# Both tiles of queries of a head pair in one attention step, with the softmax inverses on GpSimd

## The chip, the cores and the metric

The kernel runs on one core of one Trainium2 chip. The metric is the device time of one execution in microseconds (us), lower is better; each kernel is run several times and the median counts. One execution is also recorded by the hardware profiler, and its rows are what this document argues from. The engines are named as the profile names them: PE is TensorE (matmuls), PEld its weight loads, DVE is VectorE, ACT is ScalarE, POOL is GpSimd, SP issues nearly all DMAs.

## The reference

The program is a small encoder trunk: 256 tokens, model width 1024, two layers, float32 inputs. An even layer mixes two kinds of attention behind one input projection; the odd layer uses dilated windows. Each is followed by a squared-ReLU MLP. The change touches the attention of the even layer:

```python
def even_mixer(xn, w_in, rpb, q_norm, w_uq, kv_norm, w_ukv, w_o, cos_r, sin_r):
    hcat = xn @ w_in
    ...
    out_a = neighbourhood_attention(a_qkv[:, :, 0], a_qkv[:, :, 1], a_qkv[:, :, 2], rpb)
    ...
    out_b = dense_attention(q, k, v, (MLA_NOPE + MLA_ROPE) ** -0.5)
    return jnp.concatenate([out_a, out_b], axis=-1) @ w_o
```

Both kinds have 8 heads. In the first (neighbourhood attention, head width 64) a query sees a window of the 4 x 64 grid and a learned bias is added to its scores. The second (latent attention) is dense, with queries and keys of width 96 and values of width 64. For both, each row of scores passes through a softmax:

```python
sc = jnp.einsum('bqhd,bkhd->bhqk', qi, k, preferred_element_type=jnp.float32) * scale
p = jax.nn.softmax(sc, axis=-1)
return jnp.einsum('bhqk,bkhd->bqhd', p.astype(v.dtype), v)
```

## The kernel before

Activations lie as columns of tokens (256 tokens, two tiles of 128). A float32 product is made of three matmuls of a rounded type: every operand is split into a high part and the rest (`split`, L167 a cast on ScalarE, L168 a difference on VectorE), and `mm3` (L171 to L173) multiplies high by high, high by low and low by high. All weights are read from memory once, 1 MB pieces at a time, on SP's queue, and split in quarters (`whi`, `wlo`) up to two weights ahead of their use. So ScalarE and VectorE have a steady load of splits beside everything else.

The even layer's attention is woven into the projections around it. `attention` returns a list of side steps; the loop at the end of `even` runs the main steps (queries and keys of head pairs 1 to 3, the latent queries, keys and values, and the output projection) and after each of them as many side steps as its share of cost allows. This order, as written, is what the scheduling layer starts from; it then sets each engine's order, moving an instruction back where it does not expect its operands in time. Each engine runs its order strictly.

There are 16 items: kind 0 (neighbourhood) and then kind 1 (latent), for each of four head pairs, for each of two tiles of queries. One item passes through three functions:

- `scores`: the scores of two heads into PSUM banks of tag `w` (of which there are four). Kind 0 uses `two_heads` (L180): the two heads have 64 rows each and sit side by side in the array; each takes a bank of its own of which half is used. Kind 1 uses `mm3`. Then, on VectorE, one instruction a head scales the scores, adds the bias (kind 0, L668; kind 1 has none, L671) and takes the minimum of their negation; on ScalarE one exp a head with its sum `z` (L673); on VectorE the inverse of both sums (L674); on ScalarE one scaling a head (L676).
- `turn_probs`: four transpositions on TensorE (L683) into a bank, and a copy out of it (L685, on ScalarE or VectorE).
- `mix`: the products with the values (L697), two heads in halves of 64 columns of the array, into a bank, then a `split` of 128 columns for the output projection.

The side steps of the items are set in the order scores(n), turn_probs(n - 1), mix(n - 2), with two empty steps after the first scores. So an item's transpositions are the fourth side step behind its scores, and its mix comes four behind them.

The bias of an item (256 KB) is loaded by `load_bias` into one of two buffers, two items ahead; its DMA waits on SP's queue until the item that had the buffer has read it.

Of the kernel before, what the change touches and what calls it, by code (L numbers as in the profile page):

```python
# [16 lines left out]
F32 = mybir.dt.float32  # L17
F32R = mybir.dt.float32r
AF = mybir.ActivationFunctionType
ALU = mybir.AluOpType  # L20
# [3 lines left out]
P = 128  # L24
D = 1024
KT = D // P
T = 256
NT = T // P
# [5 lines left out]
MLA_SCALE = (64 + 32) ** -0.5  # L34
# [4 lines left out]
SPLIT_AHEAD = 2  # L39
WPARTS = 4  # L40
NORM_PRIO = 300


@with_exitstack
def trunk(ctx, tc, a, out):
    nc = tc.nc
# [123 lines left out]
    def mm3(o, sh, sl, mh, ml, first, last):  # L170
        nc.tensor.matmul(o, sh, mh, start=first, stop=False)  # L171
        nc.tensor.matmul(o, sh, ml, start=False, stop=False)  # L172
        nc.tensor.matmul(o, sl, mh, start=False, stop=last)  # L173

    def two_heads(o, hi, lo, ts):

        for n, (y, z) in enumerate(((hi, hi), (hi, lo), (lo, hi))):
            for j in range(2):
                pb = slice(64 * j, 64 * j + 64)
                nc.tensor.matmul(o[j], y[pb, 0, ts], z[pb, 1, :], start=n == 0, stop=n == 2)  # L180
# [10 lines left out]
    def tok(t):  # L191
        return slice(t * P, (t + 1) * P)
# [255 lines left out]
    def even(ep):  # L448
# [200 lines left out]

        def scores(n):  # L650
            kind, t, hp = items[n]
            load_bias(n + 2)

            sb = [bank("w")[:, 0:T] for _ in range(2)] if kind == 0 else bank("w").rearrange("p (j n) -> p j n", j=2)
            s_of = lambda j: sb[j] if kind == 0 else sb[:, j]
            if kind == 0:
                two_heads(sb, *qk[hp], tok(t))
            else:
                for j in range(2):
                    h = 2 * hp + j  # L660
                    (qh, ql), (kh, kl) = mT["q"], mT["k"]
                    mm3(sb[:, j], qh[0:96, h, tok(t)], ql[0:96, h, tok(t)], kh[0:96, h, :], kl[0:96, h, :], True, True)
            pp, sn = scratch([2, T], "pp"), scratch([2, T], "sn")
            mn, z, rz = (work.tile([P, 2], F32, tag=v, name=v, bufs=3) for v in ("mn", "z", "rz"))
            for j in range(2):
                o = s_of(j)
                if kind == 0:
                    nc.vector.tensor_tensor_reduce(out=sn[:, j], in0=o, in1=biases[n][:, j, :], op0=ALU.add, op1=ALU.min,  # L668
                                                   scale=-1.0, scalar=3e38, accum_out=mn[:, j:j + 1])
                else:  # L670
                    nc.vector.tensor_scalar(sn[:, j], o, -MLA_SCALE, None, ALU.mult, ALU.min, accum_out=mn[:, j:j + 1])  # L671
            for j in range(2):
                nc.scalar.activation(pp[:, j], sn[:, j], AF.Exp, bias=mn[:, j:j + 1], scale=-1.0, accum_out=z[:, j:j + 1])  # L673
            nc.vector.reciprocal(rz, z)  # L674
            for j in range(2):
                nc.scalar.activation(pp[:, j], pp[:, j], AF.Copy, scale=rz[:, j:j + 1])  # L676
            probs[n] = pp

        def turn_probs(n):
            pp = probs.pop(n)  # L680
            pt = bank("w")
            for b in range(4):
                nc.tensor.transpose(pt[:, b * P:(b + 1) * P], pp[:, b // 2, (b % 2) * P:(b % 2 + 1) * P], ident)  # L683
            turned[n] = scratch([4, P], "pts")
            nc.any.tensor_copy(out=turned[n], in_=pt.rearrange("p (b n) -> p b n", b=4))  # L685

        def mix(n):
            kind, t, hp = items[n]
            pts = turned.pop(n)
# [4 lines left out]
            for kk in range(NT):  # L694
                for j in range(2):
                    h = 2 * hp + j
                    nc.tensor.matmul(pvo[64 * j:64 * j + 64, 0:P], v[:, kk, h * 64:(h + 1) * 64], pts[:, 2 * j + kk, :],  # L697
                                     start=kk == 0, stop=kk == NT - 1)
            split(*(z[:, hp, tok(t)] for z in mixed[kind]), pvo[:, 0:P])

        def attention():

            out = []
            for n in range(len(items) + 2):
                for fn, m in ((scores, n), (turn_probs, n - 1), (mix, n - 2)):
                    if 0 <= m < len(items):
                        out.append(lambda fn=fn, m=m: fn(m))
                if n == 0:
                    out += [lambda: None] * 2
            return out  # L710

        (ug, ut), (kg, kt) = uq_steps(), ukv_steps()
        first = qk_steps(0)
        run_all(first[:1])
        load_bias(0)
        load_bias(1)
        run_all(first[1:3])
        row = as_row(dg)
        nc.scalar.mul(both[:, 0, :], row, HD ** -0.5)
# [230 lines left out]
def _layout(i):  # L950
    f = np.ascontiguousarray
    w = i["ev_w_in"][0]
    d = {"x": f(i["x"][0][ORDER].T.reshape(KT, P, T).transpose(1, 0, 2))}
    d["w_c"] = f(w[:, 1536:].reshape(2, 4, P, 416).transpose(0, 2, 1, 3).reshape(2, P, -1))
    d["w_qk"] = f(w[:, :1024].reshape(KT, P, 2, 4, P).transpose(3, 1, 0, 2, 4).reshape(4, P, -1))
    d["w_v"] = f(w[:, 1024:1536].reshape(2, 4, P, 512).transpose(0, 2, 1, 3).reshape(2, P, -1))
    d["w_uq"] = f(i["ev_w_uq"][0].reshape(1, 2, P, 768).transpose(0, 2, 1, 3).reshape(1, P, -1))
    d["w_ukv"] = f(i["ev_w_ukv"][0].reshape(1, P, 1024))
    d["w_oe"] = f(i["ev_w_o"][0].reshape(4, 2, P, D).transpose(0, 2, 1, 3).reshape(4, P, -1))
    d["w_oo"] = f(i["od_w_o"][0].reshape(4, 2, P, D).transpose(0, 2, 1, 3).reshape(4, P, -1))  # L960

# [16 lines left out]
    d["rpb"] = f(rp.reshape(4, 2, NT, P, T).transpose(2, 0, 3, 1, 4))  # L978
# [25 lines left out]
```

## Time and profile before

| | |
|---|---|
| median of 3 runs | 767.98 us (767.9 to 768.18) |
| the profiled execution's own time | 768.55 us |
| its span, first to last instruction | 766.7 us |
| mean granted TensorE clock | 0.998 |
| matmuls in the profile | 5898 |
| even layer's attention, first scores to last mix | about 41.6 to 112 us |

The page of the profile gives each engine's busy time. A line of a group shows the program's line, engine, operation and tiles, then how often, and after the bar its busy time and the mean duration in ns. The chain that ended last is followed back from the last instruction, at each step to what released it; a piece shows its start, its share of time and how many instructions it merges. Windows show busy us of each engine in a stretch. Matmuls overlap in the pipeline, so a row's duration is longer than the spacing of matmuls, and a busy TensorE can still lose time between them.

### The profile page before, as it was taken

The page shows a single profiled execution, that of the slowest core. Times are in us where ns is not written, and L with a number is a line of the kernel's source. Part 1 is how long each engine was busy: PE and PEld are TensorE (multiplying, and loading weights), DVE is VectorE, ACT ScalarE, POOL GpSimd, SP SyncE. Part 2 cuts the span into 40 slices and gives each one's busy share as a digit, 9 for nine tenths or more (in the row PEclk, how much of TensorE's full clock was granted, in tenths as well). Part 3 has the DMA queues.
Part 4 walks back from the last instruction along what each step waited for, and adds up shares of the span by engine and source line. Part 5 has one row for each costly group of instructions (what it writes and reads, how often), then busy time and mean ns, then how long its engine had stood idle before and what let it go on. Part 6 is the DMA issues. An engine that isn't in the chain of part 4 may idle for free.

```text
span 766.7 us, 14611 instructions
## 1 busy us (share of the span) xinstructions
PE 757.2 (99%) x5898; PEld 716.6 (93%) x5898; DVE 500.8 (65%) x1028; ACT 507.5 (66%) x1078; POOL 9.5 (1%) x22
## 2 busy tenths in 40 slices
PE   8999999999999999999999999999999999999996
PEld 5998999999999999999999999999999899899895
DVE  6788858655555557877667676767749555555564
ACT  6788967444444445888988989989857454454541
POOL 0100000000000001000000000000000000000000
PEclk9999999999999999999999999999999999999999
DMA  8763334555555444643452534435454554554501
GB/s 282 302 227 132 111 110 167 173 212 167 172 212 168 170 186 149 207 160 125 167 183 104 203 110 176 159 120 184 165 194 164 172 214 165 172 213 168 178 40 55
DMA packets 22819, 129.13 MB, mean 168 GB/s; under 512 B 2913, under 2 KB 5473, under 8 KB 9825
## 3 DMA queue, kind: packets, MB, share of 16 engines
q1 hardware_dynamic: 22464, 127.94, 47.5%
q8 instruction: 46, 0.75, 0.4%
q10 hardware_dynamic: 288, 0.28, 0.1%
q14 instruction: 21, 0.16, 0.1%
HBM read 127.16 MB, written 1.05 MB: 167 GB/s over the span
## 4 chain that ended last, share of the span: by engine, by line
PE 89%; ACT 5%; DVE 2%; issue 2%; DMA 1%; SPq 0%; POOLq 0%; POOL 0%
PE acc L171 19%; PE acc L172 18%; PE acc L173 18%; PE w L171 9%; PE w L172 9%; PE w L173 9%; PE w L180 1%; DMA raw<-in_w_c 1%; ACT whi L167 1%; PE w L859 1%; PE w L683 1%; PE w L843 1%; PE w L697 1%; DVE wlo L168 1%; PE acc L868 1%
## 5 line engine op out<-in xcount | busy, mean ns | idle before, releaser
L168 DVE TENSOR_TENSOR wlo<-raw,whi 128x512 fp32r<-128x512 f32 (+3 forms) x488 | 307.5, 663 | 165.6 <-ACT whi L167 164.6
L167 ACT CAST whi<-raw 128x512 fp32r<-128x512 f32 (+3 forms) x488 | 268.7, 600 | 201.9 <-issue 173.3
L172 PE MATMUL w<-xl,whi 128*128 128x256 f32 x528 | 149.1, 282 | 0.0
L173 PE MATMUL w<-xh,wlo 128*128 128x256 f32 x528 | 149.0, 282 | 0.0
L171 PE MATMUL w<-xh,whi 128*128 128x256 f32 x528 | 148.8, 282 | 0.0
L171 PE MATMUL acc<-xh,whi 128*128 128x256 f32 x432 | 125.2, 290 | 0.0
L173 PE MATMUL acc<-xh,wlo 128*128 128x256 f32 x432 | 121.9, 282 | 0.0
L172 PE MATMUL acc<-xl,whi 128*128 128x256 f32 x432 | 121.8, 282 | 0.0
L171 PEld LDWEIGHTS w<-xh,whi 128*128 128x128 f32 x528 | 99.6, 189 | 0.6
L172 PEld LDWEIGHTS w<-xl,whi 128*128 128x128 f32 x528 | 99.3, 188 | 0.5
L173 PEld LDWEIGHTS w<-xh,wlo 128*128 128x128 f32 x528 | 99.5, 188 | 0.0
L171 PEld LDWEIGHTS acc<-xh,whi 128*128 128x128 f32 x432 | 81.4, 188 | 2.4 <-issue 1.4
L172 PEld LDWEIGHTS acc<-xl,whi 128*128 128x128 f32 x432 | 81.6, 189 | 0.0
L173 PEld LDWEIGHTS acc<-xh,wlo 128*128 128x128 f32 x432 | 81.2, 188 | 0.0
L171 PE MATMUL acc<-hh,whi 128*128 128x256 f32 x256 | 72.6, 284 | 0.0
L172 PE MATMUL acc<-hl,whi 128*128 128x256 f32 x256 | 72.4, 283 | 0.0
L173 PE MATMUL acc<-hh,wlo 128*128 128x256 f32 x256 | 72.4, 283 | 0.0
L171 PE MATMUL acc<-whi,xh 128*128 128x384 f32 (+2 forms) x160 | 57.5, 359 | 0.9 <-ACT whi L167 0.9
L172 PE MATMUL acc<-wlo,xh 128*128 128x384 f32 (+2 forms) x160 | 55.8, 349 | 0.4 <-DVE wlo L168 0.4
L173 PE MATMUL acc<-whi,xl 128*128 128x384 f32 (+2 forms) x160 | 54.9, 343 | 0.0
L171 PEld LDWEIGHTS acc<-hh,whi 128*128 128x128 f32 x256 | 49.1, 192 | 0.0
L173 PEld LDWEIGHTS acc<-hh,wlo 128*128 128x128 f32 x256 | 49.1, 192 | 0.0
(202 smaller groups left out, 1289.9 us busy)
## 6 DMA issues: line engine op xcount, KB each, us to landing
raw<-in_w SPq DMA_DIRECT2D x64, 1024.0 KB, 4.8
raw<-in_w_oqk SPq DMA_DIRECT2D x24, 1024.0 KB, 4.8
raw<-in_w_ov SPq DMA_DIRECT2D x16, 768.0 KB, 4.3
raw<-in_w_qk SPq DMA_DIRECT2D x4, 1024.0 KB, 10.5
raw<-in_w_oe SPq DMA_DIRECT2D x4, 1024.0 KB, 5.2
raw<-in_w_oo SPq DMA_DIRECT2D x4, 1024.0 KB, 4.8
bias<-in_rpb SPq DMA_DIRECT2D x8, 256.0 KB, 4.0
raw<-in_w_c SPq DMA_DIRECT2D x8, 208.0 KB, 4.7
```

What stands on the lines that cost most here:

```text
L167: a = nc.scalar.copy(hi, src).ins
L168: return a, (eng or nc.vector).tensor_tensor(lo, src, hi.bitcast(F32), op=ALU.subtract).ins
L171: nc.tensor.matmul(o, sh, mh, start=first, stop=False)
L172: nc.tensor.matmul(o, sh, ml, start=False, stop=False)
L173: nc.tensor.matmul(o, sl, mh, start=False, stop=last)
L180: nc.tensor.matmul(o[j], y[pb, 0, ts], z[pb, 1, :], start=n == 0, stop=n == 2)
L683: nc.tensor.transpose(pt[:, b * P:(b + 1) * P], pp[:, b // 2, (b % 2) * P:(b % 2 + 1) * P], ident)
L697: nc.tensor.matmul(pvo[64 * j:64 * j + 64, 0:P], v[:, kk, h * 64:(h + 1) * 64], pts[:, 2 * j + kk, :], start=kk == 0, stop=kk == NT - 1)
L843: nc.tensor.matmul(ss[j][rows, T:T + P], d["q12"][:, j, i * P + 64 * c:i * P + 64 * c + 64], d["k12"][:, j, 2 * i + c, :], start=True, sto ...
L859: nc.tensor.transpose(pt[:, b * P:(b + 1) * P], pp[:, b * P:(b + 1) * P], ident)
L868: nc.tensor.matmul(pvo[cs, 0:P], d["v0"][:, kk, cs], turned[i, j][:, kk, :], start=kk == 0, stop=False)
```

## The change

An item is now a kind and a head pair, eight in all, each with both tiles of queries. `scores` computes both tiles' scores into two banks before the reductions, exps and scalings, tile by tile. The inverse of the sums is a power of -1 on GpSimd instead of VectorE's reciprocal. `turn_probs` still takes one tile. `mix` takes both tiles into one bank, with one `split` of 256 columns. The side steps of an item are: scores with the preceding item's mix beside it, two empty steps, the two tiles' transpositions, an empty step. The bias of a head pair's both tiles (512 KB) is one DMA into one buffer, one item ahead.

```diff
+BIASBUFS = 1
...
+    mone = const.tile([P, 1], F32, name="mone")
+    nc.gpsimd.memset(mone, -1.0)
...
-        items = [(0, t, hp) for hp in range(4) for t in range(NT)] + [(1, t, hp) for hp in range(4) for t in range(NT)]
+        items = [(kind, hp) for kind in range(2) for hp in range(4)]
...
-            if n < 8:
-                _, t, hp = items[n]
-                biases[n] = ep.tile([P, 2, T], F32, tag="bias", name="bias", bufs=2)
-                nc.sync.dma_start(biases[n], a["rpb"][t, hp])
+            if n < 4:
+                biases[n] = ep.tile([P, NT, 2, T], F32, tag="bias", name="bias", bufs=BIASBUFS)
+                nc.sync.dma_start(biases[n], a["rpb"][n])
...
-            load_bias(n + 2)
+            load_bias(n + BIASBUFS)
...
-                two_heads(sb, *qk[hp], tok(t))
+                sb = [two(bank("w")) for _ in range(2)]
+                s_of = lambda t, j: sb[j][:, t]
+                for t in range(NT):
+                    two_heads([s_of(t, j) for j in range(2)], *qk[hp], tok(t))
             else:
+                sb = [two(bank("w")) for _ in range(NT)]
+                s_of = lambda t, j: sb[t][:, j]
...
+            for t in range(NT):
+                pp, sn = scratch([2, T], "pp"), scratch([2, T], "sn")
...
+                for j in range(2):
+                    nc.scalar.activation(pp[:, j], sn[:, j], AF.Exp, bias=mn[:, t, j:j + 1], scale=-1.0, accum_out=z[:, t, j:j + 1])
+                nc.gpsimd.tensor_tensor(rz[:, t], z[:, t], mone.broadcast_to([P, 2]), op=ALU.pow)
+                for j in range(2):
+                    nc.scalar.activation(pp[:, j], pp[:, j], AF.Copy, scale=rz[:, t, j:j + 1])
...
-            nc.vector.reciprocal(rz, z)
...
-            pvo = bank("acc" if n < 6 else "w")
+            pvo = bank("acc" if n < 3 else "w")
+            for t in range(NT):
+                pts = turned.pop((n, t))
...
-            split(*(z[:, hp, tok(t)] for z in mixed[kind]), pvo[:, 0:P])
+            split(*(z[:, hp, :] for z in mixed[kind]), pvo[:, 0:T])
...
-            for n in range(len(items) + 2):
-                for fn, m in ((scores, n), (turn_probs, n - 1), (mix, n - 2)):
...
+            for n in range(len(items)):
+                out += [lambda n=n: (scores(n), mix(n - 1) if n else None), wait, wait,
+                        lambda n=n: turn_probs(n, 0), lambda n=n: turn_probs(n, 1), wait]
+            return out + [lambda: mix(len(items) - 1)]
```

The change moves instructions on every engine between the first scores and the last mix; ahead of them and behind them TensorE's order is the same, 225 and 4864 matmuls.

VectorE at the first scores, before: `q` are the queries and keys of the next head pair, times their factor, `qk_l` their low part; L668 with `sn,mn` are the reductions of the two heads' scores, each with a second row that reads the minimum out.

```order
L576 TENSOR_TENSOR q_545<-acc,both 128x512
L668 ISA sn,mn<-w,bias 128x256
L668 ISA mn 128x1
L668 ISA sn,mn<-w,bias 128x256
L668 ISA mn 128x1
L168 TENSOR_TENSOR qk_l<-q_545,qk_h 128x512
```

And after, where the reductions are L676:

```order
L579 TENSOR_TENSOR q_545<-acc,both 128x512
L171 TENSOR_TENSOR wlo<-raw,whi 128x256
L676 ISA sn,mn<-w,bias 128x256
L676 ISA mn 128x1
L676 ISA sn,mn<-w,bias 128x256
L676 ISA mn 128x1
L171 TENSOR_TENSOR qk_l<-q_545,qk_h 128x512
```

A piece of a weight's split has moved ahead of the reductions; the second tile's four rows follow right behind `qk_l`.

ScalarE in the late, latent items, before: L673 the exps of two heads, L676 their scalings, `whi` a piece of a weight, `obh` the cast of a finished mix.

```order
L676 ACTIVATE pp<-pp,rz 128x256 x2
L673 ACTIVATE pp,z<-sn,mn 128x256 x2
L167 CAST whi<-raw 128x512
L167 CAST obh<-w 128x128
L676 ACTIVATE pp<-pp,rz 128x256 x2
L167 CAST whi<-raw 128x512
```

After, at the item of head pair 1 (L681 the exps, L684 the scalings):

```order
L681 ACTIVATE pp,z<-sn,mn 128x256 x3
L684 ACTIVATE pp<-pp,rz 128x256 x2
L681 ACTIVATE pp,z<-sn,mn 128x256
L170 CAST obh<-w 128x256
L684 ACTIVATE pp<-pp,rz 128x256 x2
L170 CAST whi<-raw 128x512 x4
```

The two tiles' exps and scalings, which stood apart with casts between them, now stand together, and the second tile's first exp has moved ahead of the first tile's scalings.

TensorE in the late items, before: `ident,pp` are the transpositions of a tile, `pts,vml` a mix, `oah,whi` and the like the output projection.

```order
L683 MATMUL w<-ident,pp 128x128 x4
L697 MATMUL w<-pts,vml 64x128 x4
L171 MATMUL acc<-oah,whi 128x256
L172 MATMUL acc<-oal,whi 128x256
L173 MATMUL acc<-oah,wlo 128x256
```

After, the second tile of the item of head pair 1; `kh,qh` and the like are already the next item's scores:

```order
L691 MATMUL w<-ident,pp 128x128 x2
L174 MATMUL w<-kh,qh 128x256
L175 MATMUL w<-kl,qh 128x256
L691 MATMUL w<-ident,pp 128x128 x2
L176 MATMUL w<-kh,ql 128x256
```

A tile's four transpositions, which stood together, are here two and two, by head, among the following item's scores, and that item's mix of 8 matmuls (16 as the profile counts them) comes behind all of its 12 scores.

More of the change, by code (lines that the diff above doesn't have):

```diff
@@ L650, in scores @@
         def scores(n):
-            kind, t, hp = items[n]
-            load_bias(n + 2)
-            sb = [bank("w")[:, 0:T] for _ in range(2)] if kind == 0 else bank("w").rearrange("p (j n) -> p j n", j=2)
-            s_of = lambda j: sb[j] if kind == 0 else sb[:, j]
+            kind, hp = items[n]
+            load_bias(n + BIASBUFS)
             if kind == 0:
-                two_heads(sb, *qk[hp], tok(t))
-            else:
-                for j in range(2):
-                    h = 2 * hp + j
-                    (qh, ql), (kh, kl) = mT["q"], mT["k"]
-                    mm3(sb[:, j], qh[0:96, h, tok(t)], ql[0:96, h, tok(t)], kh[0:96, h, :], kl[0:96, h, :], True, True)
@@ L663, in scores @@
[L663 to L680, printed above, removed]
+                sb = [two(bank("w")) for _ in range(2)]
+                s_of = lambda t, j: sb[j][:, t]
@@ new lines, in scores @@
+            mn, z, rz = (work.tile([P, NT, 2], F32, tag=v, name=v, bufs=3) for v in ("mn", "z", "rz"))
+            for t in range(NT):
+                pp, sn = scratch([2, T], "pp"), scratch([2, T], "sn")
+                for j in range(2):
+                    at = mn[:, t, j:j + 1]
+                    if kind == 0:
+                        nc.vector.tensor_tensor_reduce(out=sn[:, j], in0=s_of(t, j), in1=biases[n][:, t, j, :], op0=ALU.add, op1=ALU.min,
+                                                       scale=-1.0, scalar=3e38, accum_out=at)
+                    else:
+                        nc.vector.tensor_scalar(sn[:, j], s_of(t, j), -MLA_SCALE, None, ALU.mult, ALU.min, accum_out=at)
+                for j in range(2):
+                    nc.scalar.activation(pp[:, j], sn[:, j], AF.Exp, bias=mn[:, t, j:j + 1], scale=-1.0, accum_out=z[:, t, j:j + 1])
+                nc.gpsimd.tensor_tensor(rz[:, t], z[:, t], mone.broadcast_to([P, 2]), op=ALU.pow)
+                for j in range(2):
+                    nc.scalar.activation(pp[:, j], pp[:, j], AF.Copy, scale=rz[:, t, j:j + 1])
+                probs[n, t] = pp
@@ L681, in turn_probs @@
+        def turn_probs(n, t):
+            pp = probs.pop((n, t))
             pt = bank("w")
@@ L683, in turn_probs @@
                 nc.tensor.transpose(pt[:, b * P:(b + 1) * P], pp[:, b // 2, (b % 2) * P:(b % 2 + 1) * P], ident)
-            turned[n] = scratch([4, P], "pts")
-            nc.any.tensor_copy(out=turned[n], in_=pt.rearrange("p (b n) -> p b n", b=4))
+            turned[n, t] = scratch([4, P], "pts")
+            nc.any.tensor_copy(out=turned[n, t], in_=pt.rearrange("p (b n) -> p b n", b=4))
         def mix(n):
-            kind, t, hp = items[n]
-            pts = turned.pop(n)
+            kind, hp = items[n]
             if mixed[kind] is None:
@@ L692, in mix @@
             v = (vna, vml)[kind]
-            pvo = bank("acc" if n < 6 else "w")
[L694 to L698, printed above, removed]
-            split(*(z[:, hp, tok(t)] for z in mixed[kind]), pvo[:, 0:P])
+            pvo = bank("acc" if n < 3 else "w")
+            for t in range(NT):
+                pts = turned.pop((n, t))
+                for kk in range(NT):
+                    for j in range(2):
+                        h = 2 * hp + j
+                        nc.tensor.matmul(pvo[64 * j:64 * j + 64, tok(t)], v[:, kk, h * 64:(h + 1) * 64], pts[:, 2 * j + kk, :],
+                                         start=kk == 0, stop=kk == NT - 1)
+            split(*(z[:, hp, :] for z in mixed[kind]), pvo[:, 0:T])
         def attention():
             out = []
-            for n in range(len(items) + 2):
-                for fn, m in ((scores, n), (turn_probs, n - 1), (mix, n - 2)):
[L706 to L710, printed above, removed]
+            wait = lambda: None
+            for n in range(len(items)):
+                out += [lambda n=n: (scores(n), mix(n - 1) if n else None), wait, wait,
+                        lambda n=n: turn_probs(n, 0), lambda n=n: turn_probs(n, 1), wait]
+            return out + [lambda: mix(len(items) - 1)]
         (ug, ut), (kg, kt) = uq_steps(), ukv_steps()
@@ L714, in even @@
         run_all(first[:1])
-        load_bias(0)
-        load_bias(1)
+        for n in range(BIASBUFS):
+            load_bias(n)
         run_all(first[1:3])
```

5 lines of the change are left out of this document (4 added, 1 removed).

## The prediction

> **What bounds the kernel now.** I read the page's busy times first, then its chain of work that ended last, then the windows, then the chain piece by piece.
>
> ```profile
> PE 757.2 (99%) x5898; PEld 716.6 (93%) x5898; DVE 500.8 (65%) x1028; ACT 507.5 (66%) x1078; POOL 9.5 (1%) x22
> ...
> PE 89%; ACT 5%; DVE 2%; issue 2%; DMA 1%; SPq 0%; POOLq 0%; POOL 0%
> ...
> 60.00:80.00 20.00, 20.00 (x161) 16.76 (x161) 18.40 (x58) 18.43 (x53) 0.88 (x3) 1.00 0.24 81
> ```
>
> TensorE (PE) is the kernel: what shortens its row of matmuls shortens the time, what makes it wait lengthens it. The even layer's attention runs from 41 to 114 us. The last row is the window of 60 to 80 us in it (PE, weight loads, DVE, ACT, POOL, in us of 20): PE never stands still, but VectorE and ScalarE are 92% busy beside it and have no room for a longer path. The pieces of the chain (start, length) show where TensorE's own time is lossy:
>
> ```profile
> 41.70 0.56 PE w L180 x6
> ...
> 45.33 0.56 PE w L180 x6
> 45.89 0.32 PE acc L171
> ...
> 50.14 0.44 PE w L683 x4
> 50.57 0.59 PE acc L697 x8
> 51.16 0.32 PE acc L171
> 51.48 0.12 PE acc L172
> ...
> 60.02 0.59 PE acc L697 x8
> 60.60 0.55 PE w L180 x6
> 61.15 0.43 PE acc L171
> 61.58 0.24 PE acc L172
> ```
>
> A full 128x128 matmul of 256 columns takes 0.12 us, a transposition (L683, 128 columns) 0.44 / 4 = 0.11. Scores (L180) use halves of 64 rows, mixes (L697) halves of 64 columns, two matmuls side by side; the first full matmul behind either takes 0.32 instead of 0.12.
>
> **Term 1, a gain: fewer changes of the array's form.** A lone block of scores costs 0.56 against 3 pairs x 0.12 = 0.36, and 0.32 - 0.12 behind it: a loss of 0.40 us. A lone mix costs 0.59 against 4 pairs x 0.11 = 0.44, and again 0.20: 0.35. A mix with scores right behind it costs 0.59 + 0.55 + 0.43 against 0.44 + 0.36 + 0.24: 0.53. In TensorE's order before there are 5 lone score blocks, 14 lone mixes (one of the 16 is cut in two) and 3 such pairs: 2.0 + 4.9 + 1.6 = 8.5 us. In the order after, the blocks hold twice the matmuls, and there are 1 lone score block, 6 lone mixes and 3 pairs, scores first: 0.4 + 2.1 + 1.6 = 4.1. The count of matmuls is unchanged, so this is **-4.4 us**. No row shows a mix right behind scores; between a lone mix (0.35) and both apart (0.75) I take the other pair's 0.53, the nearest; the ends move the sum by -0.5 and +0.7.
>
> **Term 2, a loss: the way from scores to transpositions.** Before, a tile's transpositions were the fourth woven step behind its scores; now both tiles are scored at once, and the first tile's transpositions are the third step behind, the second's the fourth. What ScalarE does in between, for one tile:
>
> ```profile
> 88.52 0.51 ACT L673 ACTIVATE pp<-sn,mn 128x256 f32<-128x256 f32 x1
> 88.92 0.19 ACT L673 ACTIVATION_READ_ACCUMULATOR pp<-sn,mn 128x1 f32 x1
> 89.02 0.50 ACT L673 ACTIVATE pp<-sn,mn 128x256 f32<-128x256 f32 x1
> 89.42 0.19 ACT L673 ACTIVATION_READ_ACCUMULATOR pp<-sn,mn 128x1 f32 x1
> ...
> 90.86 0.91 ACT L676 ACTIVATE pp<-pp,rz 128x256 f32<-128x256 f32 x2
> ```
>
> An exp every 0.50 us, the pair's sums there 1.09 after its start; a scaling 0.51 for the first head, 0.91 for both. Between exps and scalings stood VectorE's inverse (L674); now it is a power on GpSimd, for which the norms' powers (L231, L198) are the nearest rows:
>
> ```profile
> L674 DVE RECIPROCAL rz<-z x16: 154/165/167, 45.4 to 106.2; 128x2 f32<-128x2 f32 x16
> ...
> L231 POOL TENSOR_TENSOR rstd<-ms,mhalf x2: 710/892/1074, 23.0 to 311.8; 128x2 f32<-128x2 f32 x2
> ...
> 26.73 0.54 POOL L198 TENSOR_TENSOR rstd<-ss,mhalf 128x1 f32<-128x1 f32 x1 [3.07 <-DVE ss L495]
> ...
> 27.31 0.16 DVE L497 TENSOR_TENSOR rstd<-rstd 128x1 f32<-128x1 f32 x1 [0.66 <-POOL rstd L198]
> 30.11 0.68 DVE L168 TENSOR_TENSOR wlo<-raw,whi 128x512 fp32r<-128x512 f32 x1
> 30.27 0.92 POOL L198 TENSOR_TENSOR rstd<-ss,mhalf 128x1 f32<-128x1 f32 x1 [3.00 <-DVE ss L495]
> ```
>
> L497 waited 0.66 us for a power of 0.54: 0.12 goes to hand it over twice. L231 has the form of the new inverse, 128x2: 0.71 and 1.07. I take 0.71 + 0.12 and a little for a busy VectorE, **0.9 us** from sums to inverses; the bounds are 0.66 and 1.07 + 0.12 = 1.2. VectorE's own took 0.16.
>
> The GPSIMD Engine Reference of the Trainium skill (Specifications) says that GpSimd shares its SBUF interfaces with VectorE and that VectorE instructions with two SBUF inputs contend with it. The rows agree: 0.54 while VectorE waited, 0.92 beside L168, whose two inputs lie in SBUF. What it would do here is the third rival.
>
> In ScalarE's order after the change (shown with the change, steps 5 and 6) two tiles are worked off in one go: one exp covers the first wait for `rz`, one cast the second.
>
> Let S be the start of a step's scores. Where the queues are free, the reductions over the scores and then the exps follow like this (scores of 45.33 above):
>
> ```profile
> 43.32 0.41 DVE L668 CUSTOM_DVE_ANT_0 sn<-w,bias 128x256 f32<-128x256 f32 x1
> ...
> 46.10 0.42 DVE L668 CUSTOM_DVE_ANT_0 sn<-w,bias 128x256 f32<-128x256 f32 x1
> ...
> 46.56 0.51 ACT L673 ACTIVATE pp<-sn,mn 128x256 f32<-128x256 f32 x1
> ```
>
> So exps start at S + 1.2, and the first tile is ready at 1.2 + 1.09 + 0.9 + 0.51 = S + 3.7, its second head 0.4 later. On ScalarE the first scaling ends at 1.2 + 1.09 + 0.9 + 0.9 = S + 4.1; the second tile's last exp and its sum take 0.6, the inverse 0.9, the scaling 0.51: S + 6.1. With latent attention's scores (six full matmuls a tile, 0.72) both are 0.35 later. TensorE comes there after the block (some 2.2 us for 12 score and 16 mix matmuls, 2.7 latent) and the matmuls counted in its order at 0.12, transpositions at 0.11.
>
> In step 5 of that order (shown with the change) the second tile's transpositions, whole before, are cut by head and lie among the next step's scores: the order itself has run out of other matmuls to put ahead of them. TensorE's waits by step, arrival against ready:
> - Step 0 (scores at 41.70, no mix yet): the reductions began at 43.32 only, because VectorE was busy; in the order a weight split of 256 columns now stands ahead of them as well (0.41 by the reduction's row of that width), and `qk_l` ahead of the second tile's. So exps start at 43.32 + 0.41 + 0.46, S + 2.5, the tile is ready at S + 5.0, and 24 matmuls bring TensorE there at S + 4.0: 1.0, and 0.2 for the second head. The second tile's exps stand behind the first scaling, TensorE comes 12 matmuls later: 0.9 more. 2.1 us.
> - Step 1: 19 matmuls cover the first tile; `qk_l` between the reductions puts the second at S + 6.7, TensorE comes at 6.3: 0.4. Step 2: second tile at S + 5.8 against 6.1, with its second head 0.5.
> - Step 5: 8 matmuls, arrival S + 3.6 against 4.05; second tile S + 5.6 against 6.45: 1.2 together. Step 6: 18 matmuls cover the first, the second is met at S + 5.8 against 6.45: 0.6. Step 7: S + 6.1 against 6.45, and 0.3 for second heads: 0.6.
> - Steps 3 and 4 lie in the window of 92%. VectorE's order puts four weight splits (0.68 each) and a rotation ahead of step 3's reductions. Worked along the queues the waits come to 3.8 us; where TensorE's other matmuls cover them, to nothing. I take the middle, 2.0.
>
> Sum: 2.1 + 0.4 + 0.5 + 2.0 + 1.2 + 0.6 + 0.6 = **+7.4 us**. With inverses of 0.66 and steps 3 and 4 free it is 2.4; with 1.2 and the full 3.8, about 12.
>
> **Term 3, nothing.** 16 inverses leave VectorE, and eight casts on ScalarE and eight differences on VectorE become part of wider ones: some 2.6 us of instructions (16 x 0.16) and about as much again, off TensorE's path; they help only steps 3 and 4, inside that term's bounds. The bias tables come as 4 loads of 512 KB into one buffer, where 8 of 256 KB went into two:
>
> ```profile
> bias<-in_rpb SPq DMA_DIRECT2D x8, 256.0 KB, 4.0
> ```
>
> A load now starts when its step's last reduction is done and is needed by the next step's first, some 7 us later; at 4.0 for half the bytes it lands after 4 to 8. Behind it on SP's queue stand loads of `w_oe`, wanted two weights later. If it lands late, VectorE's whole queue stands, up to about 1 us in each of three steps.
>
> **Sum.** -4.4 + 7.4 = +3.0 us against the profiled run's own 768.55 (span 766.7 and 1.85 around it). The median shown is 0.57 below that run; added to the median, 767.98, it gives **771.0 us**.
>
> **Rivals.**
> - *Faster: the waits are mostly covered.* For it: before, no transposition waited long, and the order after is made to put matmuls ahead where something isn't ready. Against: step 0's 24 matmuls are counted, and no power in the rows is under 0.54. It holds below 2.9 us of waits: 766.0 with the 2.4 of the low bound, 763.6 with none. Chance 0.27.
> - *Gain and loss cancel*: waits of 2.9 to 5.9 us, as with steps 3 and 4 free (5.4): about 769. Chance 0.15.
> - *Slower still: inverses slowed by VectorE*, 1.2 instead of 0.9, or bias loads late by as much. The second tile has two inverses on its way, so 0.6 more in six steps, 3.6 us: 774.6. For it speak 0.92 and 1.07; against, that reductions and copies from PSUM have at most one SBUF input. Decides once splits (L168) run beside most inverses. Chance 0.13.
> - The forecast, slower by 1.6 to 5 us: chance 0.45.
>
> That the blocks don't merge is excluded by the order.
>
> **Numbers.** Faster by over 0.2% (1.5 us, about what a measurement of this kernel can tell from no change) 0.27, same 0.15, slower 0.45 + 0.13 = 0.58. The range takes in the upper part of the faster case and the middle of the slowest, 765.0 to 774.5; some 0.10 is left below and 0.07 above.
>
> **What would show it.** After the change, mix blocks of 16 matmuls that cost no more than 1.1 us; sixteen more instructions on POOL of 0.6 to 1.1 us; ScalarE idle before scalings, released by POOL; pieces of L691 in TensorE's chain longer than 0.11 a matmul, above all in step 0. I am wrong if these waits are absent (the 4.4 then stand alone), if inverses take under 0.5, or if VectorE waits for bias loads.

## The result and the profile after

The changed kernel takes **779.09 us** (median of 4 executions, 778.76 to 780.0) against 768.08 us for the kernel before, run beside it: a ratio of 1.0145, 95% interval 1.0128 to 1.0163. It is slower by 11.0 us, where the prediction had 3.0. The profiled execution took 779.2 us, with a span of 777.2.

The page's busy times and the sums of its chain, after:

```profile
PE 758.2 (98%) x5898; PEld 717.4 (92%) x5898; DVE 496.6 (64%) x1002; ACT 508.8 (65%) x1072; POOL 22.4 (3%) x39
...
PE 78%; ACT 8%; DVE 6%; issue 3%; POOL 2%; DMA 2%; SPq 1%; POOLq 0%; DVEq 0%; ACTq 0%
```

TensorE does the same 5898 matmuls in the same busy time, but its share of the chain has fallen from 89% to 78%. The windows of 20 us (PE, weight loads, DVE, ACT, POOL, then the granted clock) say where, and the groups of waits in the attention (40 to 126 us; us in total, times, longest) say for what:

```profile
40.00:60.00 20.00, 17.80 (x155) 15.70 (x153) 12.26 (x35) 13.99 (x39) 2.77 (x4) 1.00 0.66 238
60.00:80.00 20.00, 17.03 (x133) 13.76 (x133) 12.46 (x39) 15.16 (x43) 3.70 (x8) 0.98 0.29 104
80.00:100.00 20.00, 17.80 (x148) 16.44 (x147) 13.80 (x41) 15.21 (x41) 3.41 (x3) 0.94 0.31 107
100.00:120.00 20.00, 18.57 (x159) 16.49 (x158) 11.41 (x31) 14.96 (x41) 4.18 (x5) 1.00 0.30 106
```

```profile
PE w L691 <- ACT pp L684: 5.8, 8, 1.8
PE acc L174 <- DVE r L475: 2.7, 2, 2.5
```

```profile
ACT pp L684 <- POOL rz L682: 9.3, 15, 1.7
```

In the window of 60 to 80 us VectorE and ScalarE, 92% busy before, are now at 62% and 76%: they have less to do in the same time, because they too stand and wait. ScalarE stands still 15 times, 9.3 us, at the scalings (L684) until GpSimd has the inverses. TensorE waits for those scalings at its transpositions, and once for 2.5 us at a weight matmul.

To compare kernels I took the starts of the 623 matmuls from the first scores to the 27th matmul behind the last mix, the same work in both, and set each start-to-start against the spacing of its kind where nothing waits. What is over falls into three: behind a change of the array's form; in single gaps of over 0.23 us; in all others.

| us | first score to end | changes of form | gaps over 0.23 | the rest |
|---|---|---|---|---|
| before | 73.37 | 9.56 | 0 | -0.78 |
| after | 83.68 | 4.70 | 11.50 (15 gaps) | 2.90 |
| difference | +10.31 | -4.86 | +11.50 | +3.68 |

The 10.3 us are nearly the whole growth of the span, 10.5. The prediction's gain is there in full; its loss is twice as large as forecast.

The largest gap is at step 3. VectorE and ScalarE around it, start and length:

```profile
73.47 0.51 ACT L681 ACTIVATE pp<-sn,mn 128x256 f32<-128x256 f32 x1
...
73.97 0.50 ACT L681 ACTIVATE pp<-sn,mn 128x256 f32<-128x256 f32 x1
...
75.43 0.91 ACT L684 ACTIVATE pp<-pp,rz 128x256 f32<-128x256 f32 x2 [0.38 <-POOL rz L682]
76.24 0.49 ACT L681 ACTIVATE pp<-sn,mn 128x256 f32<-128x256 f32 x1
...
76.73 0.35 ACT L610 COPY qtok<-acc 128x256 f32<-128x256 f32 x1
...
77.11 0.29 DVE L473 TENSOR_TENSOR r<-acc,cosr 128x128 f32<-128x128 f32 x1 [2.79 <-ACT qtok L610]
77.32 0.34 DVE L475 TENSOR_TENSOR r<-acc,sinr 128x64 f32<-128x64 f32 x2
...
77.81 0.41 PE L174 MATMUL acc<-whi,ch 128*128 128x384 f32 x1 [2.45 <-DVE r L475]
```

Read from below: TensorE's matmul needs an accumulator bank, which VectorE's rotation (L473, L475) still reads; the rotation waits 2.79 us for ScalarE's copy `qtok`; and that copy has nothing to do with the softmax, but stands in ScalarE's queue behind four exps and behind two scalings, which wait 0.38 us for GpSimd.

The second is at step 4, where VectorE does four weight splits in a row while GpSimd computes one inverse:

```profile
86.50 2.48 DVE L171 TENSOR_TENSOR wlo<-raw,whi 128x512 fp32r<-128x512 f32 x4
```

```profile
87.50 2.03 POOL L682 TENSOR_TENSOR rz<-z,mone 128x2 f32<-128x2 f32 x1 [9.44 <-ACT pp L681]
```

```profile
89.56 0.91 ACT L684 ACTIVATE pp<-pp,rz 128x256 f32<-128x256 f32 x2 [1.72 <-POOL rz L682]
```

The power takes 2.03 us; 13 of the 16 take 0.69. ScalarE stands for 1.72, and the transposition behind it starts 1.97 late.

And the last kind: where TensorE has stood long, it is granted a lower clock afterwards (the ninth column). Five-us windows of the changed kernel:

```profile
75.00:80.00 5.00, 2.55 (x16) 2.04 (x15) 1.95 (x6) 4.08 (x12) 1.55 (x4) 0.90 0.00 0
80.00:85.00 5.00, 5.00 (x38) 4.54 (x37) 4.38 (x12) 3.58 (x10) 0.00 (x0) 0.76 0.02 5
```

0.10 and 0.24 of 5 us are 1.7 us of TensorE's time, a part of "the rest"; about 2.0 us of it are small waits, most of them between the transpositions of a tile.

### The profile page after: what moved, and what is told of

It is laid out like the page before. It is cut to its first block, busy times and chain, and to the rows that moved or that the text cites. A ratio compares the mean times of both kernels' runs of the same rounds, so it can differ in the third digit from the quotient of the medians.

```text
span 777.2 us, 14599 instructions
## 1 busy us (share of the span) xinstructions
PE 758.2 (98%) x5898; PEld 717.4 (92%) x5898; DVE 496.6 (64%) x1002; ACT 508.8 (65%) x1072; POOL 22.4 (3%) x39
## 4 chain that ended last, share of the span: by engine, by line
PE 78%; ACT 8%; DVE 6%; issue 3%; POOL 2%; DMA 2%; SPq 1%; POOLq 0%; DVEq 0%; ACTq 0%
PE acc L174 16%; PE acc L175 16%; PE acc L176 16%; PE w L175 8%; PE w L174 8%; PE w L176 8%; DVE wlo L171 3%; ACT whi L170 2%; ACT pp L681 2%; POOL rz L682 2%; ACT pp L684 1%; PE w L866 1%; DMA raw<-in_w_v 1%; PE w L183 1%; PE w L850 1%
## 5 line engine op out<-in xcount | busy, mean ns | idle before, releaser
L175 PEld LDWEIGHTS acc<-hl,whi 128*128 128x128 f32 x256 | 49.1, 192 | 0.0
```

## The experiments

Theory, as it stood first: the way from scores to transpositions is too long for its place in the list, and the stop at GpSimd is a part of it, with what is queued behind. Rivals: the inverse on GpSimd is the whole loss (rival 1); only the distance counts, whoever computes the inverse (rival 2).

**The inverse back on VectorE.**

```diff
-                nc.gpsimd.tensor_tensor(rz[:, t], z[:, t], mone.broadcast_to([P, 2]), op=ALU.pow)
+                nc.vector.reciprocal(rz[:, t], z[:, t])
```

> The changed kernel with one line different: the inverse of the softmax sums is VectorE's reciprocal again, so GpSimd has no part in the attention. Theory (the way from the scores to the transpositions is too long for the two empty places that the list leaves, and the stop at GpSimd is one part of it; the queues behind that stop are another): the four largest waits shorten, the one of 2.62 us at step 3 and the one of 1.97 us at step 4 by 1 us or more each, the small ones by 0.3 to 0.5 us each; about 771 to 775 us. Rival 1 (the inverse on GpSimd is the whole loss): the gain of 4.86 us in the array's form is left over and the time falls below the kernel before, 763 to 766 us. Rival 2 (only the distance in the list matters, the inverse's engine does not): 778 to 779 us, the waits as they were.

Measured: 767.84 us, ratio to the kernel before 1.0000 (0.9991 to 1.0010). One line gives back 11.25 us, more than the theory allowed for; rival 2 is out. It isn't quite rival 1 either: the time stops at the kernel before, though the changes of form still cost 4.6 in place of 9.56. The scheduling layer built a new order for this kernel, as for every one below: 41 of the 623 matmuls stand elsewhere than in the changed kernel, so the 11.25 us are the line's and the new order's together.

**The inverse on GpSimd in the kernel before**, the same line the other way round.

> The kernel before with one line different: the inverse of the softmax sums is GpSimd's power, everything else (one tile of queries a step, the old list) as it was. Theory (a stop on a way that has room hides for the most part): 768.5 to 770.5 us, with waits of under 1 us at single transpositions. Rival 1 (the inverse on GpSimd is the whole loss, by itself or by contention with VectorE): 774 us or more. Rival 2 (only the distance matters): 768.0 to 768.3 us.

Measured: 770.99 us, ratio 1.0041 (1.0026 to 1.0056): 3.0 us, a little over the theory's range and far from rival 1. The stops are there all the same:

```profile
ACT pp L678 <- POOL rz L676: 8.2, 14, 1.0
```

8.2 us of ScalarE's standing cost 3.0 where one tile's softmax is done at a time, and with two tiles at a time 9.3 cost 11.25. So the loss is neither the inverse nor the merging alone, but the two together. That the single tiles have room to hide their stops in is likely; no run took it apart.

**The transpositions one place later**, with GpSimd and with VectorE's reciprocal.

```diff
-                out += [lambda n=n: (scores(n), mix(n - 1) if n else None), wait, wait,
-                        lambda n=n: turn_probs(n, 0), lambda n=n: turn_probs(n, 1), wait]
+                out += [lambda n=n: (scores(n), mix(n - 1) if n else None), wait, wait, wait,
+                        lambda n=n: turn_probs(n, 0), lambda n=n: turn_probs(n, 1)]
```

> The changed kernel with the transpositions one place later in the list of each step (three empty places behind the scores in place of two, none behind the transpositions); the inverse stays on GpSimd. Theory: a place is worth about 1.5 us of main work, so waits of under 1.5 us go and the two largest keep 0.5 to 1.1 us each, while the sums of values stand closer behind the last transposition's copy and may wait a few tenths; 768 to 771 us. Rival 1 (GpSimd's stop blocks ScalarE's queue wherever the transpositions stand): 775 us or more. Rival 2 (only the distance matters): all waits go, 763.5 to 766 us.

> Both edits at once: VectorE's reciprocal and the transpositions one place later. Theory: nearly all of the 15.2 us of waits go and the gain in the array's form stands, 763.5 to 766 us. Rival 1: as with the reciprocal alone, 763 to 766 us, so the two do not add. Rival 2: as with the later transpositions alone. If 770 us or more are left, neither the inverse nor the distance explains the loss, and the merging itself (twice the work on VectorE and ScalarE in one burst) is the cause.

Measured: 777.34 us (ratio 1.0125, 1.0110 to 1.0140), and with the reciprocal 767.57 (1.0004, 0.9994 to 1.0015). More distance gives back only 1.75 us: the theory's main part falls, and this time is what rival 1 had (775 or more). With the reciprocal both the theory and rival 1 were missed, by 1.6 us and more: the time stops at the kernel before again. Moving the transpositions moves those who wait for ScalarE, and doesn't shorten its stops:

```profile
ACT pp L684 <- POOL rz L682: 9.0, 16, 0.9
```

A new theory: **ScalarE's queue stops at the scalings, and all that stands behind them is late**, the transpositions, the copies and the next tile's exps alike.

**Occupied, not waited for.** The reciprocal feeds the scalings; GpSimd computes its power beside it into a tile that nobody reads.

```diff
-                nc.gpsimd.tensor_tensor(rz[:, t], z[:, t], mone.broadcast_to([P, 2]), op=ALU.pow)
+                nc.gpsimd.tensor_tensor(spare[:, t], z[:, t], mone.broadcast_to([P, 2]), op=ALU.pow)
+                nc.vector.reciprocal(rz[:, t], z[:, t])
```

> The changed kernel with VectorE's reciprocal for the scalings, and GpSimd's power still computed at its old place into a tile that nobody reads. It tells two ways apart in which the power on GpSimd can cost the 11.2 us that the reciprocal alone gave back. Theory (the wait: ScalarE's queue stops at the scalings until GpSimd has answered, and what is queued behind them is late): nobody waits for the power here, 767.5 to 769 us. Rival (the occupation: GpSimd beside VectorE slows VectorE's instructions or its own): 773 to 779 us.

Measured: 768.27 us, ratio 1.0006 (0.9997 to 1.0016). That is 0.4 us more than with the reciprocal alone, within the noise: GpSimd's work beside it costs next to nothing, the waiting for it does.

**The scalings later.** The inverse stays on GpSimd, and the four scalings are written into the first empty place.

```diff
+        def scale(n):
+            for t in range(NT):
+                pp, rz = probs[n, t]
+                for j in range(2):
+                    nc.scalar.activation(pp[:, j], pp[:, j], AF.Copy, scale=rz[:, t, j:j + 1])
...
-                out += [lambda n=n: (scores(n), mix(n - 1) if n else None), wait, wait,
+                out += [lambda n=n: (scores(n), mix(n - 1) if n else None), lambda n=n: scale(n), wait,
```

> The changed kernel, inverse on GpSimd, with the four scalings of a step written one place later, so that in ScalarE's queue the exponentials of the second tile stand ahead of the first tile's scalings, and the queries' copy at step 3 ahead of all four. Theory (ScalarE's queue stops at the scalings): the inverse arrives while ScalarE has other work, the wait of 2.62 us at step 3 goes, and 4 to 8 of the 11.2 us come back: 771 to 775 us. Rival (the answer itself is late for the transpositions, whatever stands in the queue): 777 to 781 us, since the first tile's scalings now come later still.

Measured: **768.18 us**, ratio 1.0003 (0.9994 to 1.0012), 10.9 of the 11.0 us back, more than expected, with the same powers on the same engine. ScalarE at step 3 now:

```profile
71.89 0.50 ACT L681 ACTIVATE pp<-sn,mn 128x256 f32<-128x256 f32 x1
72.29 0.19 ACT L681 ACTIVATION_READ_ACCUMULATOR pp<-sn,mn 128x1 f32 x1
72.38 0.35 ACT L610 COPY qtok<-acc 128x256 f32<-128x256 f32 x1
72.63 1.71 ACT L689 ACTIVATE pp<-pp,rz 128x256 f32<-128x256 f32 x4
```

```profile
ACT pp L689 <- POOL rz L682: 1.5, 3, 0.9
```

Four exps and the copy stand ahead of the scalings, and when ScalarE comes to each tile's, that tile's inverse is there. Its standing falls from 9.3 us to 1.5: 0.87 and 0.41 at step 0, where a scaling still stands between the two tiles' exps, and 0.26 at step 4, where the powers take 1.54 and 1.08 us.

**Twice the answer's length.** A second power (to the power of one) in front of the first, in the changed kernel and in the one with the later scalings.

```diff
+                nc.gpsimd.tensor_tensor(once[:, t], z[:, t], one.broadcast_to([P, 2]), op=ALU.pow)
-                nc.gpsimd.tensor_tensor(rz[:, t], z[:, t], mone.broadcast_to([P, 2]), op=ALU.pow)
+                nc.gpsimd.tensor_tensor(rz[:, t], once[:, t], mone.broadcast_to([P, 2]), op=ALU.pow)
```

> The changed kernel with a second power on GpSimd in front of the first (to the power of one, into a tile of its own, so the result is the same): each of the 16 answers comes about 0.7 us later, and nothing else is altered. Theory (ScalarE's queue stops at the scalings and has nothing to do meanwhile): ScalarE's waits for the answers grow from 9.3 us to about 20 us, and nearly all of it reaches TensorE, whose room is used up: 786 to 791 us. Rival (the first 0.7 us cost so much by tipping a few places over, and more of it costs little): 779 to 783 us.

> The same doubling in the kernel with the scalings written one place later. Theory (two exponentials with their sums, about 1 us, stand between an answer's sums and the scalings that need it, which covers one power but not two): ScalarE's waits for the answers grow from 1.5 us to 5 to 9 us, and 2 to 6 us of it reach TensorE: 770 to 774 us. Rival (what counts is when the answer is there for the transpositions, the queue does not matter): the same addition as in the kernel without the later scalings, 776 us or more.

Measured: 788.94 us (ratio 1.0268, 1.0254 to 1.0283) and 777.35 (1.0120, 1.0106 to 1.0133). ScalarE's standing in the one and in the other:

```profile
ACT pp L687 <- POOL rz L685: 20.5, 16, 1.8
```

```profile
ACT pp L692 <- POOL rz L685: 11.6, 16, 1.8
```

The first is as the theory had it: 20.5 - 9.3 = 11.2 us more of standing, 9.85 us more of time. For the second, the price is as before (10.1 us more of standing, 9.2 of time), but I had the cover too large: I took 5 to 9 us of standing, and there were 11.6, since the four powers of a step stand one behind the other on GpSimd and the second tile's wait for the first's. So the time landed at the rival's number, and what the second power adds is nearly the first kernel's 9.85, as the rival had it: this run alone doesn't part the two. Against the rival speaks that with the same powers the later scalings save 10.9 and 11.6 us. What covers a power here is some two exps' time, not the whole place. TensorE's order in the two kernels with later scalings is the same but for one matmul of 623, so here the price of standing is read without a new order of TensorE's: 9.2 us for 10.1.

**What gives the gain of 4.9 us back.** Eight kernels with VectorE's reciprocal look for it. First, the kernel before with only the mixes merged, and the changed one with the second tile's softmax one place later:

```diff
-            for n in range(len(items) + 2):
-                for fn, m in ((scores, n), (turn_probs, n - 1), (mix, n - 2)):
+            for n in range(len(items)):
+                out.append(lambda n=n: (scores(n), mix(n - 2) if n % 2 and n > 1 else None))
+                out += [lambda n=n: turn_probs(n - 1) if n else None, wait]
```

> The kernel before with only the sums of values taken for both tiles of queries at once (one block of 64-column matmuls and one split of 256 columns for two items, beside the scores of the second item); scores, softmax and transpositions one tile at a time as before, inverse on VectorE. Theory (the array's form gives its gain wherever blocks are put together, and a softmax of one tile at a time doesn't crowd ScalarE's queue): the switches cost about 6 us in place of 9.56, no new waits, 764 to 765.5 us, faster than both kernels. Rival (what the reciprocal alone and the later transpositions showed, that a merged step gives back what it gains, holds for any merging): 767.5 to 768.5 us.

```diff
+                out += [lambda n=n: (scores(n), softmax(n, 0), mix(n - 1) if n else None), lambda n=n: softmax(n, 1), wait,
```

> The changed kernel with VectorE's reciprocal and the second tile's softmax (reductions, exponentials, scalings) written one place later than the first tile's; scores and sums of values merged as in the change. Theory (what is left of the waits with the reciprocal, 3.3 us in four spots, 1.97 of it behind a burst of two tiles' exponentials and scalings on ScalarE): half of it or more goes, 765 to 766.5 us. Rival (the burst costs nothing, the second tile only comes later to its transpositions and its scores hold their bank longer): 768 to 770 us.

Measured: 767.23 us (ratio 0.9991, 0.9982 to 1.0000) and 767.50 (0.9994, 0.9985 to 1.0003): neither the theory nor the rival was hit. In the first the changes of form cost 8.25 in place of the 6 I had expected: the built order cuts its eight merged mixes into 13 blocks, drawing matmuls between the two tiles. In the second the gaps only moved, to 1.64 us at a transposition of step 2. Next, the mixes ahead of the scores and an empty place more behind the first step's scores, without and with the softmaxes apart:

```diff
-                out += [lambda n=n: (scores(n), mix(n - 1) if n else None), wait, wait,
+                out += [lambda n=n: (mix(n - 1) if n else None, scores(n)), wait, wait] + [wait] * (n == 0) + [
```

> The changed kernel with VectorE's reciprocal, the sums of values written ahead of the scores in their common place, and one more empty place behind the first step's scores. Theory (what is left of the waits is the first step's transpositions, and ScalarE's queue at step 3, where the split of the sums of values waits 1.0 us for TensorE ahead of the exponentials): both shrink, 764.5 to 767 us. Rival (the step's work on ScalarE in one burst is the limit, whatever stands first): 767.5 to 769 us.

> The same two edits on the kernel that has the second tile's softmax one place later. Theory: 764.5 to 767 us, the wait of 1.63 us at step 2 shorter and no wait at step 3. Rival: 767 to 769 us, since the second tile's transpositions stay one place behind its softmax.

Measured: 771.83 us (ratio 1.0047, 1.0034 to 1.0061) and 769.82 (1.0030, 1.0018 to 1.0041), both misses. Written first, the mixes stand in 16 and 13 blocks where there were 9, the changes of form went up from 4.6 to 7.5 and 6.2 us, and mixes now waited themselves (1.02 us at step 3). At last, the reciprocal with the later scalings; the same with the attention's list 1.31 of the main list's cost later or earlier; and the softmaxes two places apart:

```diff
-        at = -5
+        at = -6.31
```

> The changed kernel with VectorE's reciprocal and the scalings one place later. If the stop at the inverse is all that either edit takes away: 767 to 768.5 us, as each did alone. If a stop of 1 us is still felt in either: 765.5 to 767 us.

> The same with the attention's list starting one projection step later against the main list (its first steps about 2 us, its last ones hardly). Theory 1 (collisions at particular places): the wait of 1 to 2 us at step 3 changes by 1 us or more, and the time by 1 us or more either way, against the kernel that starts as before. Theory 2 (the burst itself, wherever it stands): within 0.7 us of it.

> The same with the attention's list starting one projection step earlier. Theory 1: the time changes by 1 us or more either way, not in the same way as with the later start. Theory 2: within 0.7 us.

> The changed kernel with VectorE's reciprocal, the second tile's softmax two places behind the first's, and its transpositions two places behind the first's. Theory 2 (the burst): most of the waits go, 763.5 to 766 us. Theory 1 (places): 766.5 to 769 us, the waits at other places; the second pair of banks, held two places longer by the scores, may add some.

Measured: **766.28 us** (ratio 0.9976, 0.9967 to 0.9986), 767.72 (0.9994, 0.9985 to 1.0004), 766.36 (0.9978, 0.9969 to 0.9988), 767.65 (0.9996, 0.9987 to 1.0005). The first and the third beat both kernels. The first, beside the kernel with the reciprocal alone, answers the question as far as it was answered:

| us | changes of form | gaps over 0.23 | the rest |
|---|---|---|---|
| before | 9.56 | 0 | -0.78 |
| reciprocal | 4.57 | 3.26 | 1.56 |
| reciprocal, scalings later | 4.62 | 2.18 | 0.24 |

With the reciprocal alone a gap of 1.97 us is left at step 3, the one of the `qtok` copy, here behind exps and scalings that wait for nobody:

```profile
71.74 0.90 ACT L684 ACTIVATE pp<-pp,rz 128x256 f32<-128x256 f32 x2
72.54 0.50 ACT L681 ACTIVATE pp<-sn,mn 128x256 f32<-128x256 f32 x1
...
73.03 0.35 ACT L610 COPY qtok<-acc 128x256 f32<-128x256 f32 x1
```

Most of its "rest" is the lower clock behind that gap. Later scalings let the copy through: 1.17 us and no lower clock. Shifting the list costs 1.4 us one way, as theory 1 (particular places) had it, and nothing the other, as theory 2 (the burst) had it; the softmaxes two places apart land in theory 1's range, 767.65 against 767.84 with the reciprocal alone. So it is likely, though not shown, that what is given back lies at places where ScalarE's and VectorE's queues hold other work up, and not in the burst as such. Not settled: the three gaps that remain (0.70 and 0.31 at the first transpositions of steps 0 and 1, 1.17 at step 3) and 1.0 us of small waits eat 3.2 of the 4.9 us; the other orders of the list that I tried moved gaps to other places and were no faster.

## Why the prediction was wrong

**Term 1 was right**: -4.86 measured, -4.4 forecast. The pair with scores ahead of a mix, of which no row existed, is in the chain of the kernel with reciprocal and later scalings (start, length):

```profile
57.43 0.91 PE w L183 x12
58.34 1.02 PE acc L710 x16
59.36 0.32 PE acc L174
```

0.91 + 1.02 + 0.32 against 0.72 + 0.88 + 0.12 is a loss of 0.53, the value taken from the other pair.

**Term 2 was right in sum for the steps it could follow, and failed at "steps 3 and 4".** By steps, gaps over 0.23 us:

| step | 0 | 1 | 2 | 3 and 4 | 5 | 6 | 7 |
|---|---|---|---|---|---|---|---|
| forecast | 2.1 | 0.4 | 0.5 | 2.0 | 1.2 | 0.6 | 0.6 |
| measured | 1.9 | 1.0 | 0.9 | 5.5 | 1.0 | 1.1 | 0.2 |

Without steps 3 and 4 that is 6.0 measured against 5.4. Single steps miss by up to 0.6, and that the misses cancel is luck. (The forecast's own numbers for step 5 add up to 1.3, not 1.2.) Steps 3 and 4 took 5.5, outside even the bound of 3.8, for two reasons that the runs show. The term priced the way to the *transpositions*, but the wait of 2.62 us is at a weight matmul, for a copy that is queued on ScalarE behind the softmax. From the step's first exp to that copy 3.26 us pass in the changed kernel, 2.78 with the reciprocal and 1.98 with the later scalings, and the gap goes from 2.62 to 1.97 and 1.17. So the stop at GpSimd is the smaller part of this gap; the larger is the work of two tiles that stands ahead of the copy. And one power took 2.03 us where 0.9 was taken and 1.2 was the bound; it began 1 us into a run of four splits, each with two inputs in SBUF. The forecast had the contention as a rival with 0.3 us for each inverse; in truth 13 of 16 show none and three show 1.3, 0.5 and 0.2.

**Two things were not in the sum**: the lower clock behind a long wait, 1.7 us, and small waits of some 2.0 us, most of them between transpositions, whose mean spacing is 0.163 us where it was 0.114. Behind a wait the second head's first transposition comes 0.23 us after the one before it, and that head is scaled 0.4 us after the first; but the second transposition of either head comes 0.165 us after the first as well, and why is not shown. Together: 3.0 forecast + 3.5 for steps 3 and 4 + 0.6 for the others + 1.7 + 2.0 - 0.5 for term 1 = 10.3, as measured in the attention.

**Term 3 was right.** The four bias loads land 3.4 us after their issue, where the smaller ones took 4.0, and the rival in which they are late didn't occur: VectorE waits for none of them. Over the whole run VectorE's busy time fell by 4.2 us; ScalarE's, where a part of the saving was forecast, rose by 1.3.

```profile
bias<-in_rpb SPq DMA_DIRECT2D x4, 512.0 KB, 3.4
```

The range ended at 774.5, below the sum of its own upper bounds (767.98 + 12 - 4.4 = 775.6); even that lacked the clock and what stands in ScalarE's queue.

## What to carry to other kernels

- An instruction that waits for a slow engine holds up its whole queue. Price a longer answer not by who reads the result, but by all that stands behind the waiting instruction; and before giving the work to another engine, put other work between the question and the reader. Here the second tile's exps and a copy ahead of the scalings were worth 10.9 us, as much as taking the inverse off GpSimd.
- Two changes that use the same slack are not additive: the inverse alone cost 3.0 us, the merging alone nothing, both together 11.0.
- When fewer changes of the array's form are the aim, look at TensorE's built order: for the same matmuls in 9, 13 and 16 blocks of mixes the changes of form cost 4.6, 6.2 and 7.5 us.

## What the runs showed of the hardware

**A long wait can cost twice.** The reciprocal kernel and the one with the spare power have the same wait at step 3, 1.97 us. Their windows behind it:

```profile
75.00:80.00 5.00, 5.00 (x30) 4.70 (x29) 3.82 (x9) 4.25 (x11) 0.00 (x0) 0.66 0.02 5
```

```profile
75.00:80.00 5.00, 4.57 (x47) 4.04 (x45) 4.56 (x13) 4.93 (x12) 0.00 (x0) 1.00 0.01 3
```

One was granted a clock of 0.66 for 5 us (1.7 us lost), the other the full clock, and the spans are 767.4 and 765.8. Of the reciprocal kernel's ten executions the four with a mean clock of 0.996 took 768.35 to 769.16, the six others 767.05 to 767.97. In the attention of every trace the loss comes in portions of 3.4 us at a granted clock of 0.50 (here 75.2 to 78.6 us), 1.7 us each: one in the changed kernel, two with the later transpositions, three with two powers, none where the longest wait is under 1.4 us. Between 1.4 and 2 us it follows some waits and not others: 1.43 us with the later transpositions, but not 1.42 us in the profile of the same with the reciprocal, nor the changed kernel's own 1.97 us at step 4. The Trainium skill (TensorE: Matmul & The Clock Gate, What's actually happening) has the array's clock halved after an idle window of some 3.4 us that runs freely. The portion agrees, 3.4 us at half clock; but here waits of 2 us were enough, in some executions, where the Trainium skill names a whole idle window.

**GpSimd was slowed and VectorE was not.** The four splits beside the power of 2.03 us took 2.48 us; four in a row in the reciprocal kernel, with GpSimd idle, took 2.50. The changed kernel's three slow powers (2.03, 1.20 and 0.92 us) each began while such a split was running. The two shorter ones ended 0.55 us after that split did, the longest 0.55 us after the end of the second split behind it. Where the split began after the power (45.32 and 55.24 us), the power took its 0.69. With the spare power, which starts at other times, the longest was 0.93. That GpSimd contends with VectorE instructions of two SBUF inputs is what the GPSIMD Engine Reference of the Trainium skill says (Specifications). Here it shows on one side only, as up to three times the duration.
